# The same matmuls from other addresses: token sums and tokens moved within SBUF

## The chip, the cores and the metric

One NeuronCore of one Trainium2 chip runs the whole program in one launch. The metric is the device time of one execution in microseconds; lower is better.

## The reference

A decoder trunk of two layers on 512 tokens of width 1024, all float32. Layer 0 mixes tokens with dilated sliding-window attention, layer 1 with a gated linear recurrence; each is followed by a gated feed-forward with a short causal convolution. Every sub-layer is wrapped in RMS norms.

```python
for layer in range(DEPTH):
    h = rms_norm(x, norm_mix_pre[layer])
    h = dilated_attention_mixer(h, ...) if layer % 2 == 0 else rglru_mixer(h, ...)
    x = x + rms_norm(h, norm_mix_post[layer])
    h = rms_norm(x, norm_ffn_pre[layer])
    h = conv_ffn(h, ...)              # (gelu(conv(h @ w_up)[:, :3072]) * conv(h @ w_up)[:, 3072:]) @ w_down
    x = x + rms_norm(h, norm_ffn_post[layer])
```

## The kernel before

**Split products.** Every large product is made of three matmuls. A float32 operand is split into a high part (a rounded copy, by ScalarE in line 149) and a low part (what is left, by VectorE in line 150). High times high, high times low and low times high are added up in PSUM. Weights arrive by DMA in `raw` tiles, are split into `whi` and `wlo` tiles of 2 KB per partition, and serve as the stationary operand; the moving operand is read from SBUF column by column.

**The tokens.** `hT` holds the normalised tokens of a sub-layer, features on the partitions: two tiles of 16 KB per partition, the high part `hT0` and the low part `hT1` (`new_hT`, line 439). One pair of buffers serves all four sub-layers in turn. `rows_run` (line 649), the output projection of the attention and of the recurrent layer, makes the hT that the following feed-forward layer reads. `down` (line 841), the down-projection of a feed-forward layer, makes the one that the recurrent layer reads. The attention's is made at the start (line 1657).

**Seven products.** Part of the up-projection of both feed-forward layers (9 of 12 column chunks, `seven`, line 1060) and of the strided queries and keys of the attention use a scheme with seven block products instead of eight. A chain (`chain`, line 1023) makes one 128-feature output pair in seven steps of 12 matmuls of 256 columns (line 1036). There are 18 chains in each feed-forward layer and 16 in the attention. Steps 1, 2 and 3 read blocks of hT. Steps 5, 6, 7 and 4 read sums of blocks of hT, `T[0]`, `T[1]`, `T[2]` and `T[3]`, high and low. Within a layer the steps of neighbouring chains are interleaved by a fixed table (`AT`): 1, 5, 2, the former chain's 4, 6, 3, two or three slots for other work, 7.

**Where the sums lie.** `token_sums` (line 918) makes them and borrows tiles for them: `T[0]` and `T[1]` lie in the tile of the residual stream, `x_sb`, which is kept in DRAM meanwhile. `T[2]` lies in the two `gain` tiles (in the attention its low part lies in a general tile instead). `T[3]` lies in four weight tiles.

**Layout.** The pools follow one another in SBUF. The first, `cp`, begins at byte 8,320 of each partition with `pad`, 32 bytes, which the recurrent layer uses as `twice`. After it come `ident` (512 bytes), `x_sb` (16 KB), the two gains (4 KB each) and small tiles, among them `first_w`, `c8` and `rb`. Then `hT0` and `hT1`, then weights, then the 32 general tiles (activations, staged rows), then scalars. Bytes per partition:

| tile | start | past a multiple of 128 |
|---|---|---|
| x_sb: T[0], T[1] | 8,864 | 32 |
| gains: T[2] | 25,248 and 29,344 | 32 |
| hT0, hT1 | 36,800 and 53,184 | 64 |
| raw weights | 69,568 | 64 |
| split weights: also T[3] | 94,144 on, every 2,048 | 64 |
| general tiles | 159,680 on, every 2,048 | 64 |

Other uses of hT as the moving operand: the up-projection outside the scheme (`feat`, line 592, by `mm3`, line 412) in matmuls of 512 columns, or 256 for the first chunk of a feed-forward layer; the local queries and keys; the recurrent layer's input projections. In the values of the attention (lines 1172 and 1234) hT is the stationary operand.

Of the kernel before, what the change touches and what calls it, by code (L numbers as in the profile page):

```python
# [11 lines left out]
F32 = mybir.dt.float32  # L12
F32R = mybir.dt.float32r
# [5 lines left out]
P = 128  # L19
S = 512  # L20
D = 1024
KD = D // P
# [5 lines left out]
BUCKETS = 32  # L28
# [5 lines left out]
RAW_BUFS = 3  # L34
GEN_BUFS = 32
TOE_BUFS = 2
CP_PAD = 8
WARM = 5
SEVEN = range(3, 12)
TAIL, REST = 16, range(20, 24)  # L40
# [43 lines left out]
def kernel(  # L84
# [25 lines left out]
    nc = tc.nc  # L110
    ctx.enter_context(tc.manual_schedule())
    cp = ctx.enter_context(tc.tile_pool(name="cp", bufs=1))
    twice = cp.tile([P, CP_PAD], F32, tag="pad", name="pad")
    htp = ctx.enter_context(tc.tile_pool(name="htp", bufs=1))
    wp = ctx.enter_context(tc.tile_pool(name="wp", bufs=HALVES))
    gp = ctx.enter_context(tc.tile_pool(name="gp", bufs=GEN_BUFS))
# [6 lines left out]
    def nm(s):  # L123
        uid[0] += 1
        return f"{s}{uid[0]}"
# [4 lines left out]
    def psum(s="ps"):  # L130
        return pp.tile([P, 512], F32, tag="ps", name=nm(s))

    def small(cols, s="s"):
        return sp.tile([P, cols], F32, tag=f"s{cols}", name=nm(s))
# [7 lines left out]
    def gain(src, layer, eng=nc.gpsimd):  # L142
        g = cp.tile([P, D], F32, tag="gain", name=nm("gain"), bufs=2)
        row = src[layer]
        eng.dma_start(g, bass.AP(tensor=row.tensor, offset=row.offset, ap=[[0, P], [1, D]]))
        return g
# [8 lines left out]
    sides, first_w, first_y, one = [], [], [], []  # L155
# [186 lines left out]
    def chunk():  # L342
        i = state["next"]
        state["next"] += 1
        return i

    def take(i, j):
        while (i, j) not in units:
            before = state["live"]
            pump(1)  # L350
            assert before != state["live"], (i, j, state)
        return units[i, j]

    def done(n=2):
        state["live"] -= n

    def side(steps, delay=1):
        sides.append([delay, steps])
# [18 lines left out]
    def tick(length=1):  # L377
        for s in list(sides):
            s[0] -= length
            if s[0] <= 0:  # L380
                try:
                    s[0] = next(s[1])
                except StopIteration:
                    sides.remove(s)
        if not state["hold"]:
            pump(1 if state["even"] or state["live"] >= HALVES - 4 else 2)
# [23 lines left out]
    def mm3(dst, l, r, start, stop):  # L410
        for n, (a, b) in enumerate(PASSES):
            mm(dst, l[a], r[b], start=start and n == 0, stop=stop and n == 2)  # L412
# [18 lines left out]
    def root_table():  # L431

        one = small(1)
        nc.scalar.activation(one, ident[:, 0:1], AF.Sqrt)
# [1 line left out]
    def halves(ap):  # L436
        return [ap[:, 0:512], ap[:, 512:1024]]

    def new_hT():
        return tuple(htp.tile([P, KD, S], F32R, tag=f"hT{i}", name=nm(f"hT{i}")) for i in range(2))  # L440

    def turned(*parts):

# [140 lines left out]
    def norms(t, banks, post_g, pre_g, hT):  # L584
        state["hold"] = t >= 2
        postnorm(t, banks, post_g, hT is None)
        if hT is not None:
            yield from prenorm(t, hT, pre_g, 3 if t == 3 else 4)
        if t == 3:
            state["hold"] = False  # L590
# [57 lines left out]

    def rows_run(nchunks, A, prep, seq, order, post, pre, eng):
        post_g = gain(*post, eng)  # L650
        pre_g, hT = (gain(*pre, eng), new_hT()) if pre is not None else (None, None)
        W, banks = {}, {}
        left = {}
        uses = {k: 8 for k in range(2 * nchunks)}
        root_table()

        def product(t, i, k, cols, start, stop):
            w = take(*W[k // 2][k % 2])
            mm3(
                banks[t][i][:, cols],  # L660
                [a[:, t * P : (t + 1) * P] for a in A[k]],
                [v[i][:, 0, cols] for v in w],
                start,
                stop,
            )

        for tiles, chunks in order:
            for c in chunks:
                if c not in W:
                    i = chunk()  # L670
                    W[c] = (i, 0), (i, 1)
                last = len(tiles) == 1
                if last:
                    prep(seq.index(2 * c) + 4)
                    loop = [[(tiles[0], i, kk) for i in range(2) for kk in range(2)]]
                else:
                    loop = [[(t, i, kk) for t in tiles for i in range(2)] for kk in range(2)]
                for n, part in enumerate(loop):
                    prep(seq.index(2 * c + n) + 3)
                    for t, i, kk in part:  # L680
                        k = 2 * c + kk
                        if t not in banks:
                            banks[t] = [psum("acc"), psum("acc")]
                            left[t] = [2 * nchunks, 2 * nchunks]
                        n = left[t][i]
                        left[t][i] -= 1
                        uses[k] -= 1
                        product(t, i, k, slice(0, 512), n == 2 * nchunks, n == 1)
                        if not uses[k]:
                            done()  # L690
                    for t in tiles:
                        if left[t] == [0, 0]:
                            side(norms(t, banks[t], post_g, pre_g, hT))
                    tick()
        return hT
# [9 lines left out]
    def column_rows(parts):  # L705

        st = gen(s="st")
        at = 0
        for src, c in parts:
            nc.sync.dma_start(st[at : at + c, :P], src)  # L710
            at += c
        return st, at

    def columns(st, n):

        ps = psum("cols")
        nc.tensor.transpose(ps[:, :n], st[:n, :P], ident[:n, :n])
        res = cp.tile([P, n], F32, tag=f"cols{n}", name=nm("cols"), bufs=4 if n == 96 else 1)
        nc.vector.tensor_copy(res, ps[:, :n])
        return res  # L720

    ffn_cols, lru_cols = {}, []

    def feature_columns():
        v = lambda r: r.rearrange("(j p) -> j p", p=P)
        v2 = lambda r: r.rearrange("n (j p) -> (n j) p", p=P)
        rows = [
            column_rows(
                [(v(lru_conv_w[0, k]), 8) for k in range(4)]
                + [(v(lru_conv_b[0]), 8), (v2(lru_ga_b[0]), 8), (v2(lru_gx_b[0]), 8), (v(lru_lambda[0]), 8)]  # L730
            )
        ]
        yield 1
        for layer in range(2):
            cw, cb = ffn_conv_w[layer], ffn_conv_b[layer]
            rows.append(column_rows([(v(cw[0]), 48), (v(cw[1]), 48)]))
            rows.append(column_rows([(v(cw[2]), 48), (v(cb), 48)]))
            yield 1
        cl = columns(*rows[0])
        lam = cl[:, 56:64]  # L740
        la, z, sv, s2, qv = (small(8) for _ in range(5))
        c8 = cp.tile([P, 8], F32, tag="c8", name="c8")
        nc.vector.scalar_tensor_tensor(z, lam, -1.0, lam, op0=ALU.mult, op1=ALU.min)
        nc.scalar.activation(z, z, AF.Exp)
        nc.vector.tensor_scalar(sv, z, 2.0, None, op0=ALU.add)
        nc.vector.reciprocal(sv, sv)
        nc.vector.tensor_tensor(sv, sv, z, op=ALU.mult)
        nc.vector.tensor_tensor(s2, sv, sv, op=ALU.mult)
        nc.vector.tensor_scalar(qv, s2, 1.0 / 17.0, None, op0=ALU.mult)
        for n in (15, 13, 11, 9, 7, 5, 3):  # L750
            nc.vector.scalar_tensor_tensor(qv, qv, 1.0 / n, s2, op0=ALU.add, op1=ALU.mult)
        nc.vector.scalar_tensor_tensor(qv, qv, 1.0, sv, op0=ALU.add, op1=ALU.mult)
        nc.vector.tensor_scalar(la, lam, 0.0, 8.0, op0=ALU.min, op1=ALU.mult)
        nc.vector.scalar_tensor_tensor(c8, qv, -16.0, la, op0=ALU.mult, op1=ALU.add)
        nc.vector.tensor_scalar(cl[:, 56:64], c8, -1.0, None, op0=ALU.mult)
        nc.vector.tensor_scalar(twice, c8, 2.0, None, op0=ALU.mult)
        lru_cols.extend([cl, c8])
        yield 1
        for layer in range(2):
            ffn_cols[layer] = tuple(columns(*rows[1 + 2 * layer + i]) for i in range(2))  # L760
            yield 1
# [765 lines left out]


    def lru(hT, post, pre):
        cl, c8 = lru_cols  # L1530

        xb, xs = [], []

# [170 lines left out]
    hT = attention(hT, (norm_mix_post, 0), (norm_ffn_pre, 0))  # L1704
    hT = ffn(0, hT, (norm_ffn_post, 0), (norm_mix_pre, 1))
    hT = lru(hT, (norm_mix_post, 1), (norm_ffn_pre, 1))
    ffn(1, hT, (norm_ffn_post, 1), None)
    drain()
# [27 lines left out]
```

## Time and profile before

| | |
|---|---|
| median of 3 runs | 1415.4 us (1415.21 to 1416.23) |
| profiled execution, first to last instruction | 1413.6 us |
| TensorE matmuls | 1403.6 us busy, 8741 matmuls |
| TensorE weight loads | 1266.1 us busy |
| VectorE | 1122.2 us busy |
| ScalarE | 792.4 us busy |
| GpSimd | 224.9 us busy |
| mean granted clock of TensorE | 0.999 |

The profile is of one execution; the span runs from its first instruction to its last, and the page gives no other time for that execution. Engines overlap, so busy times do not add up to the span. Matmuls are pipelined: the length of one (283 ns for 256 columns) is longer than the spacing from one start to the next, and it is the spacing that makes the time of a stretch of matmuls. In the rows, `ps<-T,whi` is a matmul that writes the PSUM tile ps from the moving tile T and the stationary tile whi; the leading figure of a timeline row is its start in us.

### The profile page before, as it was taken

What the parts mean: (1) busy time and instruction counts of PE and PEld (TensorE: products, weight loads), DVE (VectorE), ACT (ScalarE), POOL (GpSimd) and SP (SyncE); (2) the same over time, 40 slices, a digit from 0 to 9 for tenths busy, and PEclk for the clock granted to TensorE, in tenths of its full rate; (3) what the DMA queues carried; (4) which work ended last, traced back from release to release, by engine and by line L of the source; (5) the groups of instructions that cost most, each with busy time, mean ns of one, the idle gap of its engine ahead of it and who ended that gap; (6) DMA issues with size and microseconds to landing.
All of it is one profiled execution on the core that took longest, in us unless ns stands there. A gap on an engine that the chain in (4) does not pass through costs nothing.

```text
span 1413.6 us, 23534 instructions
## 1 busy us (share of the span) xinstructions
PE 1403.6 (99%) x8741; PEld 1266.1 (90%) x8741; DVE 1122.2 (79%) x2201; ACT 792.4 (56%) x1646; POOL 224.9 (16%) x344
## 2 busy tenths in 40 slices
PE   9999999999999999999999999999999999999998
PEld 7888999999998899999999888888898999999886
DVE  6675897887866889998888758769789999888843
ACT  7343555453536555666566645589455666665641
POOL 0341332231310102222110001000101212111000
PEclk9999999999999999999999999999999999999999
DMA  7544464655665545767554632431444767664511
GB/s 228 179 144 114 120 181 140 185 157 168 162 201 172 168 157 112 157 152 167 121 142 97 214 129 90 134 120 61 146 130 99 171 134 164 156 129 116 180 56 60
DMA packets 171883, 201.92 MB, mean 143 GB/s; under 512 B 10560, under 2 KB 141080, under 8 KB 171512
## 3 DMA queue, kind: packets, MB, share of 16 engines
q1 hardware_dynamic: 123064, 153.34, 34.1%
q0 software_dynamic: 47856, 46.02, 17.8%
q8 instruction: 69, 1.13, 0.3%
q10 hardware_dynamic: 848, 1.05, 0.2%
q14 instruction: 46, 0.38, 0.1%
HBM read 181.41 MB, written 18.96 MB: 142 GB/s over the span
## 4 chain that ended last, share of the span: by engine, by line
PE 90%; DVE 4%; ACT 4%; issue 1%; DMA 0%; POOL 0%; DVEq 0%; ACTq 0%
PE ps L1036 36%; PE acc L412 25%; PE ps L412 17%; PE v L1234 7%; PE v L1172 1%; DVE wlo L150 1%; DVE xb L1539 1%; PE O L1446 1%; PE S L1380 1%; PE S L1328 1%; ACT whi L149 1%; ACT sig L1560 1%; PE tr L502 1%; PE O L412 0%; ACT sig L1579 0%
## 5 line engine op out<-in xcount | busy, mean ns | idle before, releaser
L150 DVE TENSOR_TENSOR wlo<-raw,whi 128x512 fp32r<-128x512 f32 x620 | 408.4, 685 | 119.0 <-ACT whi L149 117.1
L149 ACT ACTIVATE whi<-raw 128x512 fp32r<-128x512 f32 x620 | 367.0, 625 | 151.8 <-PE acc L412 48.0
L1036 PE MATMUL ps<-T,whi 128*128 128x256 f32 x1664 | 303.6, 283 | 0.7 <-DVE ps L1054 0.7
L412 PE MATMUL ps<-hT,whi 128*128 128x512 f32 (+1 forms) x1088 | 288.2, 354 | 0.0
L1036 PEld LDWEIGHTS ps<-T,whi 128*128 128x128 f32 x1664 | 259.0, 190 | 5.0 <-DVE ps L1054 1.1
L1036 PE MATMUL ps<-T,wlo 128*128 128x256 f32 x832 | 233.2, 280 | 0.0
L1036 PE MATMUL ps<-hT,whi 128*128 128x256 f32 x1248 | 230.5, 283 | 0.0
L412 PEld LDWEIGHTS ps<-hT,whi 128*128 128x128 f32 x1088 | 190.9, 189 | 26.3
L1036 PEld LDWEIGHTS ps<-hT,whi 128*128 128x128 f32 x1248 | 195.8, 191 | 2.6
L412 PE MATMUL ps<-hT,wlo 128*128 128x512 f32 (+1 forms) x544 | 191.5, 352 | 0.0
L1036 PE MATMUL ps<-hT,wlo 128*128 128x256 f32 x624 | 176.7, 283 | 0.0
L186 POOL DMA_DIRECT2D raw<-in_ffn_w_up_dram x72 | 92.8, 1318 | 422.4 <-DVE wlo L150 303.5
L1036 PEld LDWEIGHTS ps<-T,wlo 128*128 128x128 f32 x832 | 158.4, 190 | 0.0
L412 PE MATMUL acc<-whi,ahi 128*128 128x512 f32 x352 | 137.8, 391 | 0.0
L412 PE MATMUL acc<-whi,alo 128*128 128x512 f32 x352 | 137.4, 390 | 0.1
L412 PE MATMUL acc<-wlo,ahi 128*128 128x512 f32 x352 | 137.2, 390 | 0.0
L1036 PEld LDWEIGHTS ps<-hT,wlo 128*128 128x128 f32 x624 | 119.5, 191 | 0.0
L412 PEld LDWEIGHTS ps<-hT,wlo 128*128 128x128 f32 x544 | 102.9, 189 | 14.0
L1045 ACT ACTIVATE part<-ps 128x256 f32<-128x256 f32 x156 | 59.0, 378 | 97.2 <-PE ps L1036 93.9
L1234 PE MATMUL v<-whi,hT 128*128 128x512 f32 x320 | 106.6, 396 | 0.0
L777 DVE SCALAR_TENSOR_TENSOR u<-ps,cols,u 128x511 f32<-128x511 f32 x120 | 89.3, 746 | 5.5 <-ACT u L773 3.4
L773 ACT ACTIVATE u<-ps,cols 128x512 f32<-128x512 f32 x60 | 46.2, 774 | 63.0 <-DVE ps L1049 48.9
(206 smaller groups left out, 2143.7 us busy)
## 6 DMA issues: line engine op xcount, KB each, us to landing
raw<-in_ffn_w_up_dram SPq DMA_DIRECT2D x48, 1024.0 KB
raw<-in_attn_w_qkv_dram SPq DMA_DIRECT2D x67, 512.0 KB
raw<-in_ffn_w_up_dram POOLq DMA_DIRECT2D x72, 256.0 KB, 4.8
raw<-in_ffn_w_down_dram SPq DMA_DIRECT2D x14, 1024.0 KB
dw<-in_ffn_w_down_dram SPq DMA_DIRECT2D x40, 256.0 KB
raw<-in_lru_w_in_dram SPq DMA_DIRECT2D x8, 1024.0 KB
turned<-T POOLq DMA_DIRECT2D x26, 256.0 KB, 2.6
ft<-turned POOLq DMA_DIRECT2D x104, 64.0 KB, 4.6
```

The source lines that it names most:

```text
L149: nc.scalar.activation(hi, raw, AF.Copy)
L150: nc.vector.tensor_tensor(lo, raw, hi.bitcast(F32), op=ALU.subtract)
L186: nc.gpsimd.dma_start(to, src, accum_op=ALU.add)
L412: mm(dst, l[a], r[b], start=start and n == 0, stop=stop and n == 2)
L502: nc.tensor.transpose(ps[:, k * P : (k + 1) * P], xs[i][:, k * P : (k + 1) * P], ident)
L773: nc.scalar.activation(u, ps, AF.Identity, scale=own[:, j : j + 1], bias=cc[:, 48 + j : 49 + j])
L777: nc.vector.scalar_tensor_tensor(u[:, d:], ps[:, : S - d], wc, u[:, d:], op0=ALU.mult, op1=ALU.add)
L1036: mm(dst, W[wa][0][:, k, :], right[n](ha, k), start=n in (1, 5) and k == q == 0, stop=k == 3 and q == 2, skip_group_check=True,)
L1045: later(1, lambda: nc.scalar.activation(to, dst, AF.Copy))
L1172: mm(banks[t], hT[a][:, k, t * P : (t + 1) * P], W[b][k % 2][:, 0, :], start=u == n == 0, stop=u == 3 and n == 5,)
L1234: mm(bank, hT[a][:, k, t * P : (t + 1) * P], W[b][k % 2][:, 0, :], start=(k, a, b) == (0, 0, 0), stop=(k, a, b) == (KD - 1, 1, 0),)
L1328: mm(Sp[a // 2][:, o + lo : o + 256], q[hh][:, a * P : (a + 1) * P], k[hh][:, k0 : (a + 1) * P], start=True, stop=True)
```

## The change

The pad goes, so that x_sb and the gains start 32 bytes lower (8,832, 25,216 and 29,312, all multiples of 128). `twice` moves into the buffer of `rb` and `c8` into that of `first_w`, both of which are done with by then, so the first pool is 64 bytes shorter in all. The two parts of hT become one tile that is 64 bytes longer than both were. It starts at 36,736, a multiple of 128. The feed-forward layers' hT uses it from its first byte (36,736 and 53,120); the attention's and the recurrent layer's use it from 64 bytes on, which is where hT was before (36,800 and 53,184). Everything behind keeps its address. No instruction is added or taken away, and the order of the work stays.

```diff
-CP_PAD = 8
+NEAR = 16
...
-    twice = cp.tile([P, CP_PAD], F32, tag="pad", name="pad")
...
-    def new_hT():
-        return tuple(htp.tile([P, KD, S], F32R, tag=f"hT{i}", name=nm(f"hT{i}")) for i in range(2))
+    def new_hT(near=False):
+
+        both = htp.tile([P, 2 * KD * S + NEAR], F32R, tag="hT", name=nm("hT"))
+        at = 0 if near else NEAR
+        both = both[:, at : at + 2 * KD * S].rearrange("p (i k t) -> p i k t", i=2, k=KD)
+        return both[:, 0], both[:, 1]
...
-        pre_g, hT = (gain(*pre, eng), new_hT()) if pre is not None else (None, None)
+        pre_g, hT = (gain(*pre, eng), new_hT(True)) if pre is not None else (None, None)
...
-        c8 = cp.tile([P, 8], F32, tag="c8", name="c8")
+        c8 = cp.tile([P, KD], F32, tag="first_w", name="c8")
+        twice = cp.tile([P, 3, BUCKETS], F32, tag="rb", name="twice")[:, 0, 0:8]
...
-        lru_cols.extend([cl, c8])
+        lru_cols.extend([cl, c8, twice])
...
-        cl, c8 = lru_cols
+        cl, c8, twice = lru_cols
```

## The prediction

> **What bounds the kernel now.** I read the page's busy line first, then the chain of work that ended last, then the table of waits for TensorE, and last the timeline of TensorE inside one feed-forward layer.
>
> ```profile
> span 1413.6 us, 23534 instructions
> ...
> PE 1403.6 (99%) x8741; PEld 1266.1 (90%) x8741; DVE 1122.2 (79%) x2201; ACT 792.4 (56%) x1646; POOL 224.9 (16%) x344
> ...
> PE 90%; DVE 4%; ACT 4%; issue 1%; DMA 0%; POOL 0%; DVEq 0%; ACTq 0%
> PE ps L1036 36%; PE acc L412 25%; PE ps L412 17%; PE v L1234 7%; PE v L1172 1%; DVE wlo L150 1%; DVE xb L1539 1%; PE O L1446 1%; PE S L1380 1%; PE S L1328 1%; ACT whi L149 1%; ACT sig L1560 1%; PE tr L502 1%; PE O L412 0%; ACT sig L1579 0%
> ```
>
> TensorE is busy for 99% of the span and holds 90% of the chain. Line 1036, the matmuls of the seven-product scheme (256 columns each), is the largest piece of it.
>
> ```profile
> PE warm L1655 <- DVE one L1700: 1.5, 1, 1.5
> PE ps L1036 <- DVE ps L1054: 0.7, 1, 0.7
> PE v L1172 <- ACT whi L149: 0.3, 1, 0.3
> PE tr L513 <- DMA x_sb<-in_x_dram: 0.3, 1, 0.3
> PE v L1172 <- DVE wlo L150: 0.2, 1, 0.2
> ```
>
> All of TensorE's waits together are 3.0 us. So the end is set by the spacing of the matmuls, and a nanosecond on each of a few thousand of them comes straight out of the time. The span is the profiled execution's; the median of the runs is 1415.4 us, 1.8 us more. I make the sum against 1413.6 and add 1.8 back.
>
> How fast do they follow one another? Here is the timeline of TensorE, the first row of each step of 12 matmuls (start in us first), and then the twelve 512-column ones behind them:
>
> ```profile
> 595.77 0.40 PE L1036 MATMUL ps<-T,whi 128*128 128x256 f32 x2
> ...
> 597.19 0.40 PE L1036 MATMUL ps<-hT,whi 128*128 128x256 f32 x2
> ...
> 598.62 0.40 PE L1036 MATMUL ps<-T,whi 128*128 128x256 f32 x2
> ...
> 600.03 0.40 PE L1036 MATMUL ps<-hT,whi 128*128 128x256 f32 x2
> ...
> 601.47 0.40 PE L1036 MATMUL ps<-T,whi 128*128 128x256 f32 x2
> ...
> 602.91 0.40 PE L1036 MATMUL ps<-T,whi 128*128 128x256 f32 x2
> ...
> 604.33 0.40 PE L1036 MATMUL ps<-hT,whi 128*128 128x256 f32 x2
> ...
> 605.76 0.40 PE L412 MATMUL acc<-whi,whi 128*128 128x512 f32 x1
> ...
> 607.15 0.39 PE L412 MATMUL acc<-whi,whi 128*128 128x512 f32 x1
> ...
> 608.51 0.40 PE L1036 MATMUL ps<-T,whi 128*128 128x256 f32 x2
> ```
>
> By the order of the steps (products 7, 1, 5, 2, 4, 6, 3) the first, third and sixth step read the sums T[2], T[0] and T[1], which lie in the gain and x_sb tiles. They take 1.42, 1.41 and 1.42 us: 118.05 ns a matmul. The fifth reads T[3], which lies among the weights: 1.44 us, 120.0 ns. The three hT steps take 1.43, 1.44 and 1.43 us: 119.4 ns. The same instruction on the same kind of data is 1.95 ns quicker where the sums lie. The grouped rows agree, in the length of one matmul behind the wlo load:
>
> ```profile
> L1036 PE MATMUL ps<-T,wlo 128*128 128x256 f32 x832 | 233.2, 280 | 0.0
> ...
> L1036 PE MATMUL ps<-hT,wlo 128*128 128x256 f32 x624 | 176.7, 283 | 0.0
> ```
>
> What differs is the address. Adding up the tiles in the order of the kernel's pools (8,320 bytes lie ahead of the first), x_sb starts at 8,864, the gains at 25,248 and 29,344, hT at 36,800 and 53,184, weights at 94,144 and on. Past the last multiple of 128 the weights, T[3] and hT stand at 64, T[0] to T[2] at 32. So a tile that is read against weights at the same place in 128 bytes costs 120 ns, one 32 bytes from that place 118.
>
> **The change part by part.** (1) The sums' homes go from 32 to 0 in 128, which is 64 from the weights' place. Matmuls that read them: T[0] and T[1], 52 chains x 2 steps x 12 = 1,248; T[2] in the feed-forward layers 36 x 12 = 432; T[2] in the attention only its high part (8 of 12), 16 x 8 = 128. Together 1,808 of the 2,496 on T in line 1036. (2) The feed-forward hT goes from 64 to 0 in 128, also 64 from the weights. Matmuls: 36 chains x 3 steps x 12 = 1,296, and the first up-projection chunk in column halves 2 x 192 = 384, so 1,680 of 256 columns; and 8 tiles x 24 x 2 layers = 384 of 512 columns. (3) The hT of the attention and the recurrent layer and all weights stay where they are.
>
> No row shows a distance of 64, so I bound it. From below: 48 matmuls of 512 columns stand in the chain at
>
> ```profile
> 68.68 10.93 PE ps L412 x48
> ```
>
> 227.7 ns each; less 120.0 that leaves 107.7 ns for 256 columns more, which I take as the least a spacing can be. From there the sum is 1,808 x 10.3 + 1,680 x 11.7 + 384 x 12 = 18.6 + 19.7 + 4.6 = 43 us less. From above: the sums lose what they have now, 1,808 x 1.95 = 3.5 us more. A place can also hurt: of the twelve 512-column matmuls above the first six take 1.39 us and the last six 1.36, 5 ns apiece by where their tiles lie; on the 384 that is 1.9 us more. I take the straight line through the two rows I have, 0 apart 120.0 and 32 apart 118.05, to 64 apart: 116.1. It is nearest to the measured step and far from the floor. Sums: 1,808 x 1.95 = 3.5 us less. hT: 1,680 x (119.4 - 116.1) = 5.5 us less. The 384 of 512 columns I leave at nothing: 3.3 ns (1.3 us) less on one side, 1.9 us more on the other.
>
> (4) VectorE and ScalarE read and write the same tiles at the new places. Splits into the sums' homes against splits into weights:
>
> ```profile
> L150 DVE TENSOR_TENSOR wlo<-raw,whi 128x512 fp32r<-128x512 f32 x620 | 408.4, 685 | 119.0 <-ACT whi L149 117.1
> ...
> L150 DVE TENSOR_TENSOR T<-B,T 128x512 fp32r<-128x512 f32 x24 | 15.6, 685 | 2.4 <-ACT T L149 2.1
> ```
>
> 685 ns at either place, so nothing. (5) c8 takes first_w's place and twice takes rb's. Their writes on VectorE now wait for the last readers there:
>
> ```profile
> L756 DVE TENSOR_SCALAR pad<-c x1: 164/164/164, 98.9 to 98.9; 128x8 f32<-128x8 f32 x1
> ...
> L1124 POOL COPY row<-rb x34: 173/180/201, 39.8 to 46.7; 8x1 f32<-8x1 f32 x6, 8x2 f32<-8x2 f32 x5, 8x3 f32<-8x3 f32 x3, 8x16 f32<-8x16 f32 x2
> ...
> L529 DVE SCALAR_TENSOR_TENSOR hT<-T,first_w,hT x8: 348/349/352, 23.4 to 26.4; 128x128 fp32r<-128x128 f32 x8
> ```
>
> Those end at 46.7 and 26.4 us, 52 us ahead, so the wait is over when it is met. Behind it on VectorE queue the column copies and the weight splits; without that cover they would start late, and TensorE with them. (6) Both parts of hT are one tile, so the first write of a new hT waits for the readers of both old parts. The last readers of the two parts are neighbours in one triple of matmuls, a whole projection earlier: nothing; were it tracked as one piece, the low part's writes would follow the high part's, which they read anyway. No queue, DMA or order changes.
>
> What could be late next is VectorE, in one whole chain step of the layer:
>
> ```profile
> 595.93:605.92 9.99, 9.99 (x86) 9.99 (x85) 9.14 (x15) 5.37 (x12) 1.10 (x2) 1.00 0.34 60
> ...
> 546.00:776.00 230.00, 230.00 (x1694) 219.28 (x1693) 201.00 (x323) 143.88 (x268) 42.47 (x33) 1.00 0.62 139
> ```
>
> VectorE (third busy figure) has 201 of 230 us, so TensorE may gain up to 12% there before it is overtaken; 2% passes through. The sum: 1413.6 - 3.5 - 5.5 = 1404.6, and with 1.8 around it 1406.4 us.
>
> **The rivals.** *The address does nothing.* Then 280 against 283 comes from which memory region the sums lie in, and the kernel stays at 1415.4. For it: T[0] to T[2] differ from T[3] in region as well as in place. Against it: hT and T[3] lie in regions 41 KB or more apart and show 119.4 and 120.0 ns. The Trainium skill speaks for this rival: "TensorE: Matmul & The Clock Gate", Part 2: What happens when you issue a matmul, gives TensorE two independent read ports, so that loading the next weights takes nothing from the running matmul; by that rule the sum would be zero. The steps of 118.05 and 120.0 ns do not follow it.
>
> *A place is good only when it is off the 64-byte grid.* Then T at 32 was the lucky one, 0 and 64 are alike, hT gains nothing and the sums fall to 120.0 ns: 3.5 us more, 1418.9 us. It decides as soon as the T steps show 1.44 us. With 5 ns on the 384 matmuls it is 1420.8. For it: the spacings at 64 are steady at 120 while those at 32 scatter. Against it: nothing in the trace stands at 0 in 128.
>
> *The collision goes away altogether.* Halfway to the floor, 112 ns: 1,808 x 6 + 1,680 x 7.4 = 10.8 + 12.4 = 23.2 us less, 1392. For it: 32 bytes already give 2 ns; against it: the T steps at 32 are nowhere near 1.34 us.
>
> **How the numbers follow.** A measurement of this kernel can tell about 0.2% (2.8 us) from no change. Forecast (1400 to 1412): 0.44. Collision gone (1385 to 1399): 0.14. Nothing by address: 0.20. Only off the grid: 0.22. Of the forecast and of the last rival I put 0.01 each inside that band, where the effect comes out smaller than the rows say. So faster is 0.43 + 0.14 = 0.57, same 0.20 + 0.02 = 0.22, slower 0.21. The range from 1393 to 1419.5 leaves out half of the large gain and the tail of the loss. The likeliest case by itself: 1400 to 1412.
>
> **What would show it.** Steps of T at 1.39 us and hT steps of a feed-forward layer at 1.39 to 1.40 where they were 1.42 and 1.43; T[3] still 1.44 us; hT steps of the attention unchanged. The 84-matmul pieces of the chain, 9.99 us now, at 9.8. The forecast is wrong if the T steps are at 1.44 us, if hT's stay, or if the 512-column matmuls on hT lengthen; TensorE waiting on VectorE would show the gain given back.

## The result

The changed kernel takes 1407.6 us (median of 5 runs) against 1415.4 us before: a ratio of 0.994, with an interval of 0.9928 to 0.9952. The forecast was 1406.4 us. The page of the profiled execution, busy times first:

```profile
span 1405.1 us, 23534 instructions
...
PE 1395.4 (99%) x8741; PEld 1256.1 (89%) x8741; DVE 1122.2 (80%) x2201; ACT 791.2 (56%) x1646; POOL 225.5 (16%) x344
```

The span is 8.5 us shorter and TensorE's busy time 8.2 us; VectorE's is the same to a tenth. The matmuls are as many as before and closer together. TensorE's waits are still below 3 us:

```profile
PE warm L1659 <- DVE one L1704: 1.5, 1, 1.5
PE ps L1040 <- DVE ps L1058: 0.7, 1, 0.7
PE tr L516 <- DMA x_sb<-in_x_dram: 0.3, 1, 0.3
```

The groups of matmuls, by line and shape (busy time, then mean length of one). Four rows from before:

```profile
L1036 PE MATMUL ps<-T,whi 128*128 128x256 f32 x1664 | 303.6, 283 | 0.7 <-DVE ps L1054 0.7
L1036 PE MATMUL ps<-hT,whi 128*128 128x256 f32 x1248 | 230.5, 283 | 0.0
L412 PE MATMUL ps<-hT,whi 128*128 128x512 f32 x704 | 218.4, 392 | 0.0
...
L412 PE MATMUL ps<-hT,wlo 128*128 128x512 f32 x352 | 137.2, 390 | 0.0
```

And after. Line 1040 is now the seven-product scheme and line 411 the split products:

```profile
L1040 PE MATMUL ps<-T,whi 128*128 128x256 f32 x1664 | 300.6, 281 | 0.7 <-DVE ps L1058 0.7
L1040 PE MATMUL ps<-T,wlo 128*128 128x256 f32 x832 | 232.9, 280 | 0.0
L1040 PE MATMUL ps<-hT,whi 128*128 128x256 f32 x1248 | 226.0, 280 | 0.0
L411 PE MATMUL ps<-hT,whi 128*128 128x512 f32 x704 | 219.6, 393 | 0.0
L1040 PE MATMUL ps<-hT,wlo 128*128 128x256 f32 x624 | 174.7, 280 | 0.0
...
L411 PE MATMUL ps<-hT,wlo 128*128 128x512 f32 x352 | 137.9, 392 | 0.0
```

The wlo row of hT with 256 columns, 283 ns before, is at 280, and the busy times of T and hT there are down. The 512-column rows on hT went the other way (218.4 to 219.6 us and 137.2 to 137.9). These rows mix hT that moved with hT that did not.

For sums over all matmuls I took, from the trace, the time from each matmul's start to the next one's, sorted by where its moving tile lies, and compared the two kernels matmul by matmul:

| matmuls | number | before, ns | after, ns | change, us |
|---|---|---|---|---|
| 256 columns on the feed-forward hT | 1,680 | 119.8 | 115.8 | -6.8 |
| 256 columns on the moved sums | 1,808 | 118.3 | 116.5 | -3.1 |
| 512 columns on the feed-forward hT | 384 | 227.6 | 233.1 | +2.1 |
| 512 columns, down-projection work inside the scheme, whi stationary | 320 | 230.4 | 227.8 | -0.8 |
| T[3], the other hT, all else | | | | +0.1 |

The fourth line was not in the forecast: none of those tiles moved.

### The profile page after: what moved, and what is told of

The parts are those of the page before. It is cut to its first block, busy times and chain, and to the rows that moved or that the text cites. A ratio compares the mean times of both kernels' runs of the same rounds, so it can differ in the third digit from the quotient of the medians.

```text
span 1405.1 us, 23534 instructions
## 1 busy us (share of the span) xinstructions
PE 1395.4 (99%) x8741; PEld 1256.1 (89%) x8741; DVE 1122.2 (80%) x2201; ACT 791.2 (56%) x1646; POOL 225.5 (16%) x344
## 4 chain that ended last, share of the span: by engine, by line
PE 78%; ACT 4%; DVE 4%; issue 1%; DVEq 0%; ACTq 0%
PE ps L1040 34%; PE acc L411 25%; PE ps L411 11%; PE v L1238 6%; DVE xb L1543 1%; DVE wlo L149 1%; PE O L1450 1%; PE S L1384 1%; ACT whi L148 1%; ACT sig L1564 1%; PE tr L505 1%; ACT sig L1583 0%; ACT a L1581 0%; ACT xhi L148 0%; ACT th L1582 0%
## 5 line engine op out<-in xcount | busy, mean ns | idle before, releaser
L1040 PE MATMUL ps<-hT,whi 128*128 128x256 f32 x1248 | 226.0, 280 | 0.0
L411 PEld LDWEIGHTS ps<-hT,whi 128*128 128x128 f32 x1088 | 189.6, 188 | 27.7
L1040 PEld LDWEIGHTS ps<-hT,whi 128*128 128x128 f32 x1248 | 192.9, 189 | 2.6
L411 PE MATMUL acc<-whi,alo 128*128 128x512 f32 x352 | 137.2, 390 | 0.2
```

The costliest lines, as they stand in the source:

```text
L1040: mm(dst, W[wa][0][:, k, :], right[n](ha, k), start=n in (1, 5) and k == q == 0, stop=k == 3 and q == 2, skip_group_check=True,)
```

## The experiments

All diffs are against the changed kernel. "Distance" is how far the weights' place lies beyond the moving tile's.

**Only the sums moved.**

```diff
-        pre_g, hT = (gain(*pre, eng), new_hT(True)) if pre is not None else (None, None)
+        pre_g, hT = (gain(*pre, eng), new_hT()) if pre is not None else (None, None)
```

> Only the sums move (T[0] to T[2] at 0 past a multiple of 128, which is 64 away from the weights' place); every hT stays 64 past, at the weights' place. Theory A (each matmul pays by the place of its own moving tile against that of the weights): the 1,808 matmuls on the moved sums keep the 116.5 ns that they have in the changed kernel (118.3 before), 3.1 us less than before, 1412.3 us; hT steps back at 119.8 ns and the 512-column matmuls on hT at 228. Theory B (the two must move together, since the steps alternate and a step's gain hangs on the tile that was read before it): sums at 118 or more, less than 1 us gained, 1414.5 us or above.

1410.1 us, ratio to before 0.996 (0.9946 to 0.9974): quicker than either theory said (1412.3 and 1414.5). The sums stand at 116.2 ns (3.7 us less than before). The gain is larger than that, because hT's matmuls, whose tiles lie as before, take 1.0 us less and the 512-column ones on whi 0.5.

**Only the feed-forward hT moved.** The pad is back, so the sums lie at 32 again; c8 and first_y take buffers that are free, to keep all other addresses.

```diff
+    twice = cp.tile([P, 8], F32, tag="pad", name="pad")
...
-        c8 = cp.tile([P, KD], F32, tag="first_w", name="c8")
-        twice = cp.tile([P, 3, BUCKETS], F32, tag="rb", name="twice")[:, 0, 0:8]
+        c8 = cp.tile([P, 3, BUCKETS], F32, tag="rb", name="c8")[:, 0, 0:8]
...
-        y = cp.tile([P, 8], F32, tag="first_y", name="first_y")[:, 0:4]
+        y = cp.tile([P, 8], F32, tag="first_w", name="first_y")[:, 0:4]
```

> Only the feed-forward hT moves (to 0 past a multiple of 128); the sums go back to 32 past. Theory A: hT's 1,680 matmuls of 256 columns at 115.8 ns (6.8 us less than before), its 384 of 512 columns at 233 ns (2.1 us more), sums at 118.3: 1410.7 us. Theory B: hT steps at 118 or more, 1414 us or above.

1414.4 us, ratio 0.9988 (0.9979 to 0.9997): a gain of 1.2 us where theory A had 4.7. hT's 256-column matmuls stand at 117.3 ns, not at 115.8; its 512-column ones lose their 2.2 us all the same. So neither theory holds. Each tile gains by itself, but in the scheme hT's gain is whole only where the steps next to it gain too. (Of the 3.5 us missing, 2.6 us are in those matmuls and 0.6 in down-projection work inside the scheme whose tiles did not move.) The chain of work shows it in one piece of 72 matmuls, six steps at the start of the scheme in the first feed-forward layer (start, us, count). Before:

```profile
499.35 47.05 PE ps L412 x264
546.40 8.56 PE ps L1036 x72
```

Only the sums, then only hT, then both:

```profile
498.44 47.05 PE ps L411 x264
545.49 8.41 PE ps L1040 x72
```

```profile
499.83 47.21 PE ps L412 x264
547.04 8.45 PE ps L1040 x72
```

```profile
498.52 47.21 PE ps L411 x264
545.72 8.16 PE ps L1040 x72
```

The six steps lose 0.15 and 0.11 us by one part and 0.40 by both. In the trace, the hT steps that read the second 256 columns (step 3, always behind step 6) stand at 113.3 ns after a step on sums at distance 64 and at 117.7 after one on sums at 32, the 36 steps of each kernel within 0.2 ns. The stream of matmuls settles into one of a few spacings, and which one depends on the step before. The x264 piece ahead of it is the plain up-projection on hT, 120 matmuls of 256 columns and 144 of 512: it gains on the first kind and loses on the second, 0.16 us longer in all.

**Everything 64 bytes further on.**

```diff
+    twice = cp.tile([P, 16], F32, tag="pad", name="pad")[:, 0:8]
...
-        twice = cp.tile([P, 3, BUCKETS], F32, tag="rb", name="twice")[:, 0, 0:8]
```

> Every tile of the kernel lies 64 bytes further on: sums and feed-forward hT at 64 past a multiple of 128, weights and the other hT at 0. All distances between tiles are as in the changed kernel. Theory A (the distance from the weights counts): unchanged, 1407.6 us, hT 115.8 ns, sums 116.5. Theory C (the place itself counts, 0 past a multiple of 128 is good for a moving tile and 64 is not): sums and feed-forward hT at 120, the other hT and T[3] at 116 and the 512-column matmuls on weights in the down-projection at 233: above 1415 us, and the two kinds of step have changed sides.

1406.5 us, ratio 0.9935 (0.9922 to 0.9947), and row for row the changed kernel:

```profile
L1040 PE MATMUL ps<-hT,whi 128*128 128x256 f32 x1248 | 226.0, 280 | 0.0
L412 PE MATMUL ps<-hT,whi 128*128 128x512 f32 x704 | 219.6, 393 | 0.0
L1040 PE MATMUL ps<-hT,wlo 128*128 128x256 f32 x624 | 174.7, 280 | 0.0
```

The sums and hT now lie where hT lay before, and the weights at a multiple of 128. Against a shift of 64 bytes, then, the distance counts and not the place. This settles theory C.

**The weights 128, 256 and 512 bytes further from sums and hT.**

```diff
-NEAR = 16
+NEAR, MORE = 16, 32      # 64 and 128 in the other two
...
-        both = htp.tile([P, 2 * KD * S + NEAR], F32R, tag="hT", name=nm("hT"))
+        both = htp.tile([P, 2 * KD * S + NEAR + MORE], F32R, tag="hT", name=nm("hT"))
```

> hT's tile is 128 bytes longer, so the weights and all behind them lie 128 bytes further from sums and hT. Every distance in 128 stays as in the changed kernel. Theory A (only the place in 128 counts): 1407.6 us, and the steps show the same spacings. Theory F (a longer period, so that 64 and 192 away differ): the steps change by 2 ns or more, 1402 or 1413 us.

> As the run with the weights 128 bytes further on, but 256 bytes. Sums and feed-forward hT then lie 64 + 256 from the weights' place, the other hT 256. Theory J (the pattern repeats after 256 bytes): as the changed kernel, 1407.6 us, hT of 256 columns 115.8 ns, of 512 columns 233 (feed-forward) and 228 (the others). Theory K (it repeats after 512, the length of one weight slice, or more): hT's 512 columns in the attention and the recurrent layer leave 228 by 2 ns or more, the 256-column steps leave 115.8, and the time is above 1411 us.

> The same with 512 bytes. Theories J and K (it repeats after 256 or 512): as the changed kernel, 1407.6 us. Theory L (it repeats after 1,024 or 2,048, the steps of the moving tiles): spacings change as they did with 128, above 1411 us.

| shift | us | ratio | 256 columns on moved hT, ns | 512 columns on the other hT, ns |
|---|---|---|---|---|
| 0 | 1407.6 | 0.994 (0.9928 to 0.9952) | 115.8 | 228.7 |
| 128 | 1416.7 | 1.0008 (0.9999 to 1.0017) | 117.8 | 234.2 |
| 256 | 1407.0 | 0.9934 (0.9922 to 0.9947) | 115.8 | 228.7 |
| 512 | 1406.8 | 0.9941 (0.9927 to 0.9954) | 115.8 | 228.7 |

Theory A in its first form is refuted: 64 away and 192 away are not the same. With 256 the rows are back to those of the changed kernel:

```profile
L1040 PE MATMUL ps<-hT,whi 128*128 128x256 f32 x1248 | 226.0, 280 | 0.0
L411 PE MATMUL ps<-hT,whi 128*128 128x512 f32 x704 | 219.6, 393 | 0.0
```

against, with 128,

```profile
L1040 PE MATMUL ps<-hT,whi 128*128 128x256 f32 x1248 | 227.5, 280 | 0.0
L411 PE MATMUL ps<-hT,whi 128*128 128x512 f32 x704 | 220.9, 395 | 0.0
```

The pattern repeats after 256 bytes (theory J). My addresses, counted in 128, were right for this change only because none of these moving tiles lay 128 bytes or more from the weights' place in 256.

**Seven more distances.** Each of the four hT gets its own place; the sums stay at 64. The two kernels took 1421.9 and 1413.0 us (one run each), but they are to be read by spacing, since each mixes good and bad places.

```diff
-NEAR = 16
+NEAR = 24
+PLACES = [0, 4, 12, 16]      # the second run: 24, 9, 20, 7
...
-        at = 0 if near else NEAR
+        at = PLACES.pop(0)
```

> The four hT lie at four distances from the weights' place (bytes that the weights' place lies beyond hT's, in 128): attention 32, first feed-forward layer 48, recurrent layer 80, second feed-forward layer 96. The sums stay at 64. Theory A with a straight line between 0 (120 ns) and 64 (116): 118, 117, 117, 118 ns for 256 columns, and 231, 232, 232, 231 for 512. Theory D (a grid: only tiles exactly 64 away gain, all off the 64-byte grid are alike): one figure near 118 at all four, and 512 columns at about 228 at all four.

> Four more distances of hT from the weights' place, sums at 64: attention 0, first feed-forward layer 60, recurrent layer 16, second feed-forward layer 68. Theory A with a smooth course: 256 columns at 120, 116, 119, 116 ns, 512 columns at 228, 233, 229, 233. Theory D (only exactly 0 and 64 are special; all between are alike): 118 to 119 ns in both feed-forward layers, 512 columns at 232 to 235 everywhere but in the attention.

In the first of these runs the distances came out in the opposite order to what the expectation says: 96, 80, 48 and 32. Since it named the same figures forwards and backwards, it can be read either way. Mean spacing on hT by its distance in 256, the runs above included (matmuls held up by more than 15% left out):

| distance | 0 | 16 | 32 | 48 | 60 | 64 | 68 | 80 | 96 | 128 | 192 |
|---|---|---|---|---|---|---|---|---|---|---|---|
| 256 columns, ns | 119.7 | 117.2 | 118.2 | 119.1 | 120.3 | 115.5 | 115.8 | 119.0 | 117.7 | 118.7 | 117.6 |
| 512 columns, ns | 227.1 | 233.8 | 233.2 | 234.6 | 239.4 | 233.2 | 229.9 | 231.6 | 234.1 | 232.7 | 229.2 |

There is no straight line from 0 to 64 and no grid with alike points between: both theories fail. 64 and 68 are a narrow good spot for 256 columns, and four bytes on the other side of it, 60, is no better than 0 for 256 columns and the worst place of all for 512. For 512 columns nothing tried is better than 0. Neighbours differ from layer to layer, so a figure here may be off by the nanosecond or two that they make.

Outside the scheme there are pieces of 48 to 192 matmuls of one kind on hT, in which no neighbour differs. There 256 columns stand at 120.0 ns for 0 and 60, about 119.3 for 48 and 80, 118.3 for 32, 117.1 for 16 and 115.6 for 68. At 64, in the changed kernel, a piece of 48 stands at 117.8 and the next, of 120, at 113.3, so one distance can have two steady spacings. In 512 columns such pieces stand at 226.7 for 0, 233.3 for 64 and 240.0 for 60. The weights did not move in the two runs with `PLACES`, so for shifts other than 64 bytes the distance and the moving tile's own place are not told apart.

**Every hT 64 away.**

```diff
-    def new_hT(near=False):
+    def new_hT(near=True):
```

> The changed kernel with the attention's and the recurrent layer's hT at the first byte too, 64 away from the weights' place. Theory A by the spacings of the changed kernel: 768 matmuls of 256 columns 4 ns quicker (3.1 us less), 672 of 512 columns 5.5 ns slower (3.7 us more), and if a stationary hT counts like a moving one, the 576 value matmuls 5.5 ns slower (3.2 us more): 1411.4 us. Theory G (the stationary tile's place does not count for the values): 1408.2 us. Theory H (512 columns lose in the feed-forward layers for another reason than the place): 1404.5 us.

1407.5 us, ratio 0.9944 (0.9932 to 0.9957): the same as the changed kernel. The attention's and the recurrent layer's 768 matmuls of 256 columns gain 4.1 us, their 672 of 512 columns lose 4.1, and the values, which have hT as the stationary tile, lose 1.1 where I had put 3.2. Theory H is out: 512 columns lose there as well. G comes closest in the total, but its reason is not borne out: the median spacing of the 480 values made behind the first ones (line 1238) goes from 227 to 230 ns. There the stationary tile lies 64 bytes ahead of the moving one, which is 192 in 256, and at 192 the table above has 229.2. One attention piece of 240 matmuls, in the changed kernel and then here:

```profile
237.78 28.39 PE ps L1040 x240
```

```profile
239.97 27.63 PE ps L1040 x240
```

**Halves instead of 512 columns.** If 256 columns gain at this distance and 512 lose, the plain up-projection tiles should be made in halves, though that loads the weights twice.

```diff
-    def feat_tile(i, m, hT, sink):
+    def feat_tile(i, m, hT, sink, cut=S):
         ps = psum()
-        feat(take(i, m), hT, ps, 0, S)
+        for at in range(0, S, cut):
+            feat(take(i, m), hT, ps, at, at + cut)
...
-                feat_tile(i, b % 2, hT, lambda ps: begin(b, ps, j))
+                feat_tile(i, b % 2, hT, lambda ps: begin(b, ps, j), 256)
```

> In the changed kernel, the six tiles of the feed-forward up-projection that are made ahead of the seven-product scheme are computed in two halves of 256 columns instead of matmuls of 512 columns: 288 matmuls at 233 ns become 576, twice the weight loads. Theory A (256 columns profit from the distance, 512 lose): 576 at 113.3 to 116 ns, 67.2 us become 65.3 to 66.8, 0.4 to 1.9 us less, 1406.5 us. Rival (the short spacing is a matter of the chain's order of steps): 576 at 118 to 120, 0.8 to 1.9 us more, 1409 us.

1404.9 us, ratio 0.9925 (0.9912 to 0.9939), where 1406.5 was expected. The span is 2.2 us shorter than the changed kernel's; the halved tiles account for 1.9 of it, the top of what was expected for them, and the rest lies in matmuls that are as before. The piece of 47.21 us becomes

```profile
498.25 46.26 PE ps L411 x408
```

408 matmuls at 113.4 ns, the shortest spacing seen in long runs. Two halves (226.8 ns) are quicker than one matmul of 512 columns at distance 64 (233) and as quick as one at distance 0.

**All of it together**: every hT 64 away, and every `feat_tile` in halves (`cut=256` as the default, `near=True`).

> The changed kernel with every hT 64 away and every tile made on hT alone (up-projection ahead of the scheme, local queries and keys, the recurrent layer's input projections) in two halves of 256 columns; the last chunk's quarters and the values keep 512. From the runs before: attention chains 576 x (120.6 - 115.6) = 2.9 us less, the recurrent layer's halves 0.9 less, up-projection halves 2.7 less, 624 matmuls of 512 columns at 227.5 become 1,248 at 114 to 115, 0.3 to 1.6 us more, values 1.1 more: 1407.5 - 2.9 - 0.9 - 2.7 + 1.0 + 1.1 = 1403.1 us. Rival (twice the weight loads: a weight load then waits for its turn and the halves stand at 118 to 120 in the attention, where local attention lies between): 1406 us or more.

1404.2 us, ratio 0.9922 (0.991 to 0.9934), 1 us above the sum. All 4,320 matmuls of 256 columns on hT, over the four sub-layers, stand at 115.6 ns. (In the attention and the recurrent layer 648 matmuls were halved, not 624.) It and the run before beat both kernels; between these two the intervals overlap.

```profile
931.11 45.23 PE ps L411 x384
...
1030.98 46.25 PE ps L411 x408
```

The first piece, in the recurrent layer, stands at 117.8 ns, the second, in a feed-forward layer, at 113.4: the halves do not settle equally well everywhere, which is what the sum took too kindly. What decides it there is not shown.

## Why the prediction was right

- *What bounds the kernel.* TensorE's spacing, passed straight through: 8.5 us of spacing, 8.5 us of span, and VectorE busy for 1122.2 us in both. No wait of any size took its place.
- *The sums*, 3.5 us forecast, 3.1 measured. The 0 to 32 to 64 line gave 116.1 ns; it is 116.5.
- *hT with 256 columns*, 5.5 us forecast, 6.8 measured: 115.8 ns against 116.1, from 119.8 rather than the 119.4 of three steps.
- *hT with 512 columns.* I left it at nothing, with 1.9 us more as the upper end: 2.1 us more. This is the term that was mis-sized, and "the 512-column matmuls on hT lengthen" had been named as a sign that the forecast is wrong. The sign came true. The total still came out near the forecast (9.0 us less forecast, 8.5 measured) because hT with 256 columns and the down-projection work gained more than I had put, which is luck.
- *The row of 1.39 against 1.36 us*, from which the 1.9 came, I misread. I put the 5 ns down to where the tiles lie, but all twelve matmuls lie alike from their weights in 256 bytes. In all 28 such groups of twelve before, the first six, just behind a step of the scheme, stand at 231.3 ns and the next six at 226.7. That 1.9 and 2.1 agree is luck too. The distance itself shows in the piece of 144 matmuls of 512 columns on hT that stands ahead of the scheme: 226.7 ns before, 233.3 after.
- *The untouched down-projection work*, 0.8 us less, had no term. It takes its rhythm from the step before it: behind step 3 its first six matmuls go from 231.3 to 229.2 ns, behind step 7 from 231.2 to 226.7.
- *The way to the numbers.* The straight line through two rows is not what the chip does: at 16, 32, 48 and 60 bytes hT of 256 columns stands at 117.2, 118.2, 119.1 and 120.3. That the line met 64 in size is luck; that the distance matters and that 64 is better than 32 was the part that the rows carried.
- *The place in 128 bytes.* It is the distance in 256 bytes. Here that made no difference, since these moving tiles were 0, 32 or 64 bytes from the weights' place in 256 as well.
- *What would show it.* T steps at 1.39 and hT steps at 1.39 to 1.40 us were named. In the changed kernel, in the same stretch as before:

```profile
593.74 0.40 PE L1040 MATMUL ps<-T,whi 128*128 128x256 f32 x2
...
595.15 0.40 PE L1040 MATMUL ps<-hT,whi 128*128 128x256 f32 x2
...
600.89 0.40 PE L1040 MATMUL ps<-T,whi 128*128 128x256 f32 x2
...
602.27 0.39 PE L1040 MATMUL ps<-hT,whi 128*128 128x256 f32 x2
...
603.63 0.39 PE L411 MATMUL acc<-whi,whi 128*128 128x512 f32 x1
```

The first step on sums takes 1.41 us (117.5 ns), the last 1.38 (115.0), the last hT step 1.36 (113.3). The average was forecast rightly; that single steps lie on one of a few values was not. T[3] stayed at 1.44 us on the average of the feed-forward layers (120.0 ns), and the attention's hT steps are unchanged (120.4 and 120.5 ns). The 84-matmul pieces were named at 9.8 us:

```profile
593.90 9.88 PE ps L1040 x84
606.52 9.97 PE ps L1040 x84
619.23 9.82 PE ps L1040 x84
```

- *The rivals.* The address does nothing: refuted. By the rule quoted there from the Trainium skill ("TensorE: Matmul & The Clock Gate", Part 2: What happens when you issue a matmul) loading weights takes nothing from the running matmul, so the sum would have been zero. The 8.5 us, and 113.3 to 120.0 ns for one shape by the distance from the weights, do not follow it. Only off the grid: refuted, 64 is better than 32. Collision gone: true of some steps (113.3 ns), not of the average.

What makes the spacing settle where it does stays open: no run looked inside a matmul. That weight loads and moving reads meet in SBUF is only inferred, from the distance being what counts.

## What to carry over

When TensorE is the bound, compare the spacing of one kind of matmul between tiles that lie at different addresses; a nanosecond or two in a group of a thousand is an edit that costs no instruction. Treat the distance from moving tile to weights, in 256 bytes, as something to try by column count: here 64 bytes suited 256 columns and 0 suited 512, so a shared tile should be placed by its main use and the other use cut to fit. Price such edits together, because neighbouring steps share their rhythm: the parts that shortened the profiled span by 5.6 and 1.1 us alone took 8.5 off it together.

## What the runs showed of the hardware that was not expected

A matmul's spacing depended on the distance of moving and stationary tile in 256 bytes (113.3 or 117.8 ns at 64, 120.0 at 0, for 256 columns), with the same mean spacings to 0.1 ns when all tiles moved by 64. Steps settled at sharp values (113.3, 117.7, 120.0 ns for 256 columns), and the preceding step helped to choose which. Twice as many weight loads with half the columns cost nothing: two matmuls of 256 columns at 113.4 ns against one of 512 at 226.7, its best.
